# Two small joins of triangular inverses, moved from the attention's start to the stretch before it

## The chip, the cores and the metric

The program runs on one core of a Trainium2 chip, in one launch. Its engines are TensorE (PE, matmuls into PSUM; its weight loads are listed as PEld), VectorE (DVE), ScalarE (ACT), GpSimd (POOL) and SyncE (SP); 16 DMA engines move data, and transfers are issued here from SyncE's, ScalarE's and GpSimd's queues. A queue takes its instructions in order. The metric is the device time of one execution in microseconds (us); less is better.

## What is computed

One layer of a streaming encoder over 1024 tokens of width 1024: a half-step SwiGLU FFN, then two groups of heads side by side (latent attention of 4 heads, and an RWKV-7 recurrence of 8 heads of 64), then a second half-step FFN and a norm. Cut to what matters:

```python
kv = (rmsnorm(p_kv, kv_norm_g) @ w_ukv).reshape(B, S, MLA_HEADS, MLA_NOPE + MLA_V)
k_nope, v = kv[..., :MLA_NOPE], kv[..., MLA_NOPE:]
...
def step(state, inp):                      # RWKV-7, one token
    r_t, w_t, k_t, v_t, aa_t, bb_t = inp
    sa = jnp.einsum('bhvk,bhk->bhv', state, aa_t)
    state = (state * w_t[:, :, None, :] + sa[..., None] * bb_t[:, :, None, :]
             + v_t[..., None] * k_t[:, :, None, :])
    return state, jnp.einsum('bhvk,bhk->bhv', state, r_t)
```

## The kernel before

The recurrence is done in 16 chunks of 64 tokens, taken as 8 pairs of chunks. Within a chunk the recurrence needs the inverse of a 64x64 unit triangular matrix for each head. The kernel makes the two 32x32 diagonal blocks of every inverse on VectorE (`inverse32`, called once for each half of the heads), and stores them to DRAM: the first block in `tD` and, transposed, both in `fD`. The off-diagonal block of `fD` is made later, for one pair of chunks at a time, by `inverse(k, pool, p)`, called a join here. A join loads the off-diagonal block of the matrix (from `xD` into an `x21` tile) and both diagonal blocks (from `tD` into `T11`, from `fD` into `T22`), multiplies `x21` with `T11` (16 small matmuls), copies the product from PSUM into `w1`, multiplies with `T22` (16 more), copies again and stores the block into `fD`. All its transfers are issued from ScalarE's queue. The profile names tiles without their numbers, so `T11`, `T22` and the tile `T12` of the result all show as `T`, `x210` and `x211` as `x`, and `w1` as `w`; the PSUM tile is `ps_t`. Each product appears as 32 matmul instructions.

A pair's whole inverse is then loaded from `fD` into a `TF` tile by `Pair` (SyncE's queue, L1464), and `chain` uses it: a product `ps_z<-vu,m`, its copy `Z`, then the product `ps_z<-Z,TF`. The chain of a pair needs the state that the pair before leaves.

The work around the change stands in this order in the program: the latent projections (`mla_in`); `mla_up`, which makes queries, keys and, in its last two tasks, the values (`value`, PSUM tile `ps_v`, 8 blocks of tokens for each half of the value columns, copied out by ScalarE); the attention's first steps (`attend(0.4)`); the joins of pairs 0 and 1; `chain_tools` (memsets and copies on GpSimd for the chain's tiles `m`, `TF`, `wl`); and a loop over the 8 pairs, which mixes the chain of pair p, the join of pair p+2, the loads of pair p+1 and shares of the attention's steps. The attention's scores (`ps_s`) need the queries of a block as two tiles, `qh` (a ScalarE cast, L1224) and `ql` (a GpSimd subtraction, L1225).

The order of the program is a priority: a planner goes through the instructions at build time with its own cost model, and gives each engine the instruction that it takes for ready and that comes first. Pieces marked with a high priority (the chain, `inverse32`) go ahead. On the chip the order of each queue is then fixed. Tiles of one pool may lie where a pool that was closed before had its own; they wait for the last reader of what lay there.

Of the kernel before, what the change touches and what calls it, by code (L numbers as in the profile page):

```python
# [13 lines left out]
F32 = mybir.dt.float32  # L14
# [8 lines left out]
P = 128  # L23
# [47 lines left out]
def banks(k, **names):  # L71

    for n, b in names.items():
        turn = itertools.cycle(b)
        k.bank.update((x, turn) for x in n.split("_"))


def ps(k, name):
    b = next(k.bank[name])
    return k.psum.tile([P, HB], F32, name="ps_" + name, tag=f"bank{b}", bufs=1)  # L80
# [207 lines left out]
def empty():  # L288
    return [[None, None] for _ in range(ND)]
# [434 lines left out]
HL = L // 2  # L724
# [418 lines left out]
    return v(hi), v(lo)  # L1143


def mla_up(k, pool, wpool, att):

    nc = k.nc  # L1150
# [54 lines left out]
    for i, (f, h) in enumerate(tasks):  # L1205
        if i + 1 < len(tasks):
            ws.append(weights(*tasks[i + 1]))
        f(ws.pop(0), h)
    for a in range(2):
        split(k, k.krot[a], k.kr[0, a], k.kr[1, a])  # L1210
# [128 lines left out]

def inverse_tools(k, pool):  # L1340
    nc = k.nc
    k.T11, k.T22 = (pool.tile([P, 8, 2, HL], F32, name=n) for n in ("T11", "T22"))
    k.w1 = pool.tile([P, 8, HL], F32, name="w1")
    k.x21 = [pool.tile([P, 8, HL], F32, name=f"x21{i}") for i in range(2)]
    for t in [k.T11, k.T22, k.w1] + k.x21:
        nc.gpsimd.memset(t, 0.0)


# [28 lines left out]
def inverse(k, pool, p):  # L1377

    nc = k.nc
    x = k.x21[p % 2]  # L1380
    low = lambda e: slice(64 - 64 * e, 96 - 64 * e)
    high = lambda e: slice(96 - 64 * e, 128 - 64 * e)
    at = lambda e: slice(2 * p + e, 8 * NCH, NCH)
    for e in range(2):
        nc.scalar.dma_start(out=x[low(e)], in_=k.xD[at(e), :HL, HL:].rearrange("h s t -> s h t"))
        nc.scalar.dma_start(out=k.T11[low(e), :, e], in_=k.tD[at(e)].rearrange("h t c -> t h c"))
        nc.scalar.dma_start(out=k.T22[high(e), :, e], in_=k.fD[at(e), HL:, HL:].rearrange("h t c -> t h c"))

    def products(rows, lhs, rhs):
        t = ps(k, "t")[:, : 8 * HL].rearrange("p (h q) -> p h q", q=HL)  # L1390
        for h in range(8):
            for e in range(2):
                nc.tensor.matmul(t[rows(e), h], lhsT=lhs[:, h], rhs=rhs[:, h, e], start=True, stop=True)
        return t

    t = products(high, x, k.T11)
    for e in range(2):
        nc.scalar.copy(out=k.w1[high(e)], in_=t[high(e)])
    t = products(low, k.w1, k.T22)
    y = pool.tile([P, 8, HL], F32, name="T12", tag="T12", bufs=1)  # L1400
    for e in range(2):
        nc.scalar.copy(out=y[low(e)], in_=t[low(e)])
        nc.scalar.dma_start(out=k.fD[at(e), :HL, HL:].rearrange("h t c -> t h c"), in_=y[low(e)])
# [265 lines left out]
def tile_layer(ctx, tc, I, out):  # L1669
    k = Ctx()  # L1670
    setup(ctx, k, tc, I, out)
    nc = k.nc
    pool_ = lambda name, side="right": tc.tile_pool(name=name, bufs=1, side=side, reuse_waits="tile")
# [9 lines left out]
    with pool_("ffn1") as pool:  # L1683
# [5 lines left out]
        h = empty()  # L1689
# [61 lines left out]
        x = []  # L1751
# [65 lines left out]
    with pool_("winw", "left") as wpool:  # L1817
        with pool_("prep") as pool:
            win_rwkv(k, u2, pool, wpool, first)
        qkv = es_q.enter_context(pool_("qkv"))  # L1820
# [3 lines left out]

    es_a = ExitStack()
    att = es_a.enter_context(pool_("att", "left"))
    with pool_("upw") as pool:
        mla_up(k, qkv, pool, att)
    es_q.close()
    es_h.close()  # L1830
    ap = es_a.enter_context(pool_("attn", "left"))
# [6 lines left out]
    def attend(share):  # L1838
        nonlocal spent
        while steps and spent < share * total:  # L1840
            spent += cost.pop(0)
            steps.pop(0)()

    with pool_("inv", "left") as ip, pool_("chain") as pool:
        attend(0.4)
        inverse_tools(k, ip)
        inverse(k, ip, 0)
        inverse(k, ip, 1)
        chain_tools(k, pool)
        ops = [Pair(k, pool, 0)]  # L1850
        for hh in range(2):
            nc.gpsimd.memset(ops[0].sv(0, hh)[rows_of(0, hh)[1]], 0.0)
        late = None
        for p in range(NP2):
            o = ops.pop(0)
            even, odd, norm, gate = outputs(k, pool, o)
            with tc.high_priority(offset=1500):
                chain(k, pool, o, None, 0)
            if p + 2 < NP2:
                inverse(k, ip, p + 2)  # L1860
            if late:
                late()
            if p + 1 < NP2:
                ops.append(Pair(k, pool, p + 1))
            attend((p + 0.45) / 9.2)
            with tc.high_priority(offset=1500):
                chain(k, pool, o, ops[0] if ops else None, 1)
            with tc.high_priority(offset=0):
                even()
            attend((p + 1.21) / 9.2)  # L1870

            def late(odd=odd, norm=norm, gate=gate):
                with tc.high_priority(offset=0):
                    odd()
                    norm()
                    gate()

        late()
# [3 lines left out]
    h, y, u = empty(), empty(), {}  # L1882
# [3 lines left out]
    pool = Pools((own("h2b"), h0), (own("w2"), ("raw", "f8", "f9", "f10", "f11", "nwy", "nwt")))  # L1886
# [22 lines left out]
    x = []  # L1909
# [97 lines left out]
```

## Time and profile before

| | us |
|---|---|
| median of 3 runs | 2055.62 (2051.99 to 2059.74) |
| the profiled execution | 2057.89 |
| its span, first to last instruction | 2056.1 |
| TensorE busy | 1979.9 (96%) |
| VectorE busy | 1535.4 (75%) |
| ScalarE busy | 888.1 (43%) |
| GpSimd busy | 266.8 (13%) |

Times in the rows count from the start of the span. Busy time leaves out the issuing of transfers and the waiting in a queue. The granted clock (PEclk) is TensorE's as a share of 2.4 GHz: 1.00, or 0.50 for the lower level, 1.2 GHz, or a mean over a stretch.

### The profile page before, as it was taken

How to read it: one execution, taken by the hardware profiler on the slowest of the kernel's cores; microseconds unless marked ns; L12 is line 12 of the kernel's file. 1: busy time of each engine (PE TensorE's matmuls, PEld its weight loads, DVE VectorE, ACT ScalarE, POOL GpSimd, SP SyncE). 2: the span in 40 equal slices, each digit the busy share in tenths (PEclk: the TensorE clock that was granted, in tenths of full speed). 3: DMA queues.
4: the chain of work that ended last, by engine and by line, in shares of the span. 5: the costliest groups of instructions: out<-in, count | busy, mean ns of one | idle time of the engine just before them, and what ended most of it. 6: DMA issues, size and time to landing. Idle time of an engine off the chain costs nothing.

```text
span 2056.1 us, 29503 instructions
## 1 busy us (share of the span) xinstructions
PE 1979.9 (96%) x10648; PEld 1594.1 (78%) x10648; DVE 1535.4 (75%) x2939; ACT 888.1 (43%) x1678; POOL 266.8 (13%) x319
## 2 busy tenths in 40 slices
PE   6999999999999999999978899999999999999997
PEld 4788888887888777767867787787888888888887
DVE  6999997659996577896665766568566665699975
ACT  5633334335443464543344444455333333354433
POOL 1100000001000244532132323211000000000001
PEclk8999999999999999999998999999999999999999
DMA  8277753347452124656338874741223223375412
GB/s 340 78 250 236 266 177 115 111 156 248 166 175 88 67 57 122 164 136 163 88 88 175 186 184 130 266 159 42 84 85 108 103 97 106 118 269 189 144 62 83
DMA packets 222611, 302.13 MB, mean 147 GB/s; under 512 B 104704, under 2 KB 138880, under 8 KB 222464
## 3 DMA queue, kind: packets, MB, share of 16 engines
q1 hardware_dynamic: 195280, 280.16, 43.6%
q0 software_dynamic: 5120, 15.73, 2.4%
q10 hardware_dynamic: 22064, 4.35, 1.2%
q8 instruction: 84, 1.38, 0.3%
q14 instruction: 63, 0.52, 0.1%
HBM read 216.81 MB, written 80.74 MB: 145 GB/s over the span
## 4 chain that ended last, share of the span: by engine, by line
PE 71%; DVE 13%; DMA 7%; issue 4%; ACT 2%; POOL 1%; SPq 0%; DVEq 0%; ACTq 0%; POOLq 0%
PE ps_w L68 35%; PE ps_dn L68 20%; PE ps_in L68 4%; PE ps_wo L68 4%; DVE pair L62 2%; DVE wmod L140 1%; PE ps_s L68 1%; DVE T L1369 1%; PE ps_ov L1274 1%; DVE Tpr L1365 1%; DMA wmod<-w_mod 1%; PE ps_y L1519 1%; PE ps_z L1485 1%; DMA hraw<-hidD 1%; PE ps_pt L1266 1%
## 5 line engine op out<-in xcount | busy, mean ns | idle before, releaser
L68 PE MATMUL ps_w<-pair 128*128 128x512 f32 x3744 | 873.8, 394 | 13.8 <-ACT pair L61 10.2
L68 PEld LDWEIGHTS ps_w<-pair 128*128 128x128 f32 x3744 | 704.3, 188 | 180.4 <-ACT pair L61 11.5
L68 PE MATMUL ps_dn<-pair 128*128 128x512 f32 x1512 | 351.1, 393 | 1.4 <-ACT pair L61 0.6
L68 PEld LDWEIGHTS ps_dn<-pair 128*128 128x128 f32 x1512 | 283.3, 188 | 68.2 <-ACT pair L61 1.4
L68 PE MATMUL ps_in<-pair,win 128*128 128x512 f32 x960 | 239.4, 402 | 2.9 <-ACT pair L282 2.2
L61 ACT CAST pair<-raw 128x512 fp32r<-128x512 f32 x256 | 153.8, 621 | 179.6 <-PE ps_w L68 102.3
L68 PEld LDWEIGHTS ps_in<-pair,win 128*128 128x128 f32 x960 | 179.6, 190 | 50.8 <-issue 9.3
L62 DVE TENSOR_TENSOR pair<-raw,pair 128x512 fp32r<-128x512 f32 x256 | 175.5, 698 | 40.3 <-ACT pair L61 40.2
L570 DVE SCALAR_TENSOR_TENSOR h<-ps_dn,mod,h 128x512 f32<-128x512 f32 (+1 forms) x208 | 148.4, 726 | 47.4 <-PE ps_dn L68 47.4
L400 ACT COPY part<-ps_w 128x512 f32<-128x512 f32 x120 | 70.4, 586 | 210.3 <-PE ps_w L68 193.9
L61 ACT CAST pair<-draw 128x256 fp32r<-128x256 f32 x216 | 77.6, 403 | 103.3 <-DMA draw<-ffn_w_down 55.4
L61 ACT CAST pair<-hraw 128x512 fp32r<-128x512 f32 x142 | 85.6, 619 | 80.2 <-PE ps_dn L68 31.8
L62 DVE TENSOR_TENSOR pair<-hraw,pair 128x512 fp32r<-128x512 f32 x142 | 95.3, 685 | 15.5 <-ACT pair L61 15.3
L502 DVE TENSOR_TENSOR t<-ps_w,part 128x512 f32<-128x512 f32 x80 | 53.9, 686 | 55.7 <-ACT part L400 45.6
L62 DVE TENSOR_TENSOR pair<-draw,pair 128x256 fp32r<-128x256 f32 x216 | 83.6, 418 | 4.3 <-ACT pair L61 4.2
L140 DVE SCALAR_TENSOR_TENSOR wmod<-wmod,cact 128x1024 f32<-128x1024 f32 x68 | 82.8, 1220 | 4.1 <-DMA wmod<-w_mod 3.9
L68 PE MATMUL ps_dn<-pair,dh 128*128 128x512 f32 (+1 forms) x320 | 83.7, 350 | 0.0
L497 DVE TENSOR_TENSOR c<-ps_w,part 128x512 f32<-128x512 f32 x80 | 53.5, 686 | 39.3 <-ACT part L400 31.9
L68 PE MATMUL ps_wo<-pair,woh 128*128 128x512 f32 x256 | 79.3, 391 | 0.2 <-ACT woh L61 0.2
L498 ACT ACTIVATE c<-c 128x512 f32<-128x512 f32 x80 | 49.2, 630 | 40.2 <-DVE c L497 39.3
L319 POOL DMA_DIRECT2D h<-x x16 | 8.7, 549 | 436.9 <-ACT part L400 385.0
L319 POOL DMA_DIRECT2D h<-hD x16 | 8.6, 541 | 436.6 <-ACT part L400 364.6
(352 smaller groups left out, 2820.4 us busy)
## 6 DMA issues: line engine op xcount, KB each, us to landing
wmod<-w_mod SPq DMA_DIRECT2D x68, 512.0 KB, 4.4
raw<-ffn_w_gate SPq DMA_DIRECT2D x44, 512.0 KB, 4.3
raw<-ffn_w_up SPq DMA_DIRECT2D x44, 512.0 KB, 4.3
hidD<-c SPq DMA_DIRECT2D x44, 512.0 KB, 3.3
draw<-ffn_w_down SPq DMA_DIRECT2D x44, 512.0 KB, 5.0
hraw<-hidD SPq DMA_DIRECT2D x72, 256.0 KB, 3.1
hD<-h SPq DMA_DIRECT2D x32, 256.0 KB, 2.0
m3D<-m SPq DMA_DIRECT2D x32, 256.0 KB, 4.6
```

What stands on the lines that cost most here:

```text
L61: k.nc.scalar.copy(out=hi, in_=src)
L62: k.nc.vector.tensor_tensor(out=lo, in0=src, in1=hi.bitcast(F32), op=ALU.subtract)
L68: k.nc.tensor.matmul(out, lhsT=x, rhs=y, start=start, stop=stop, skip_group_check=onto)
L140: k.nc.vector.scalar_tensor_tensor(out=w, in0=w, scalar=1.0, in1=k.cact, op0=ALU.mult, op1=ALU.mult, accum_out=m)
L400: nc.scalar.copy(out=t, in_=x)
L497: nc.vector.tensor_tensor(out=c[i][:, j], in0=x, in1=y, op=ALU.add)
L498: nc.scalar.activation(out=c[i][:, j], in_=c[i][:, j], func=AF.Silu)
L502: nc.vector.tensor_tensor(out=t, in0=x, in1=y, op=ALU.add)
L570: nc.vector.scalar_tensor_tensor(out=y, in0=x, scalar=gt[:, d : d + 1], in1=y, op0=ALU.mult, op1=ALU.add)
L1266: nc.tensor.transpose(tp[:, q : q + P], pr[:, s0 + q : s0 + q + P], k.ident)
L1274: nc.tensor.matmul(x.po[:, cols], lhsT=pt[:, b * P : (b + 1) * P], rhs=k.v[b][:, cols], start=b == 0, stop=b == x.i)
L1365: nc.vector.tensor_tensor(out=v, in0=T[:, t, 0:m][:, None, :].broadcast_to([P, n, m]), in1=xp[:, t, m:][:, :, None].broadcast_to([P, n, m] ...
```

## The change

The joins of pairs 0 and 1 are called from `mla_up`, ahead of its first task for the values. The pool of their tiles is opened before `mla_up` and stays open until the attention's tiles are closed. `T11` and `T22` become one tile, `TT`: the first block is loaded into its rows `low(e)`, the second into its rows `high(e)`; in the first product the rows of `x21` that meet the second block are zero, in the second those of `w1` that meet the first. One `x21` tile serves all pairs instead of two in turn. The PSUM bank for `ps_t` is the same, 4.

```diff
-def mla_up(k, pool, wpool, att):
+def mla_up(k, pool, wpool, att, joins):
...
+        if (f, h) == (value, 0):
+            joins()
         f(ws.pop(0), h)
...
 def inverse_tools(k, pool):
     nc = k.nc
-    k.T11, k.T22 = (pool.tile([P, 8, 2, HL], F32, name=n) for n in ("T11", "T22"))
-    k.w1 = pool.tile([P, 8, HL], F32, name="w1")
-    k.x21 = [pool.tile([P, 8, HL], F32, name=f"x21{i}") for i in range(2)]
-    for t in [k.T11, k.T22, k.w1] + k.x21:
+    k.TT = pool.tile([P, 8, 2, HL], F32, name="TT")
+    k.w1, k.x21 = (pool.tile([P, 8, HL], F32, name=n) for n in ("w1", "x21"))
+    for t in [k.TT, k.w1, k.x21]:
         nc.gpsimd.memset(t, 0.0)
...
-    x = k.x21[p % 2]
+    x = k.x21
...
-        nc.scalar.dma_start(out=k.T11[low(e), :, e], in_=k.tD[at(e)].rearrange("h t c -> t h c"))
-        nc.scalar.dma_start(out=k.T22[high(e), :, e], in_=k.fD[at(e), HL:, HL:].rearrange("h t c -> t h c"))
+        nc.scalar.dma_start(out=k.TT[low(e), :, e], in_=k.tD[at(e)].rearrange("h t c -> t h c"))
+        nc.scalar.dma_start(out=k.TT[high(e), :, e], in_=k.fD[at(e), HL:, HL:].rearrange("h t c -> t h c"))
...
-    t = products(high, x, k.T11)
+    t = products(high, x, k.TT)
...
-    t = products(low, k.w1, k.T22)
+    t = products(low, k.w1, k.TT)
...
     att = es_a.enter_context(pool_("att", "left"))
+    ip = es_a.enter_context(pool_("inv", "left"))
+    inverse_tools(k, ip)
+    banks(k, t="4")
+
+    def joins():
+        for p in range(2):
+            inverse(k, ip, p)
+
     with pool_("upw") as pool:
-        mla_up(k, qkv, pool, att)
+        mla_up(k, qkv, pool, att, joins)
...
-    with pool_("inv", "left") as ip, pool_("chain") as pool:
+    with pool_("chain") as pool:
         attend(0.4)
-        inverse_tools(k, ip)
-        inverse(k, ip, 0)
-        inverse(k, ip, 1)
         chain_tools(k, pool)
```

## Rows read from the trace of the kernel before

**Rows 1.** The page, its first part: busy time, share of the span, instructions.

```profile
PE 1979.9 (96%) x10648; PEld 1594.1 (78%) x10648; DVE 1535.4 (75%) x2939; ACT 888.1 (43%) x1678; POOL 266.8 (13%) x319
```

**Rows 2.** Stretches: length, busy time of each engine (instructions), PEclk, DMA share, GB/s.

```profile
1061.00:1075.00 14.00, 12.73 (x98) 11.74 (x96) 4.39 (x7) 10.37 (x22) 0.51 (x2) 1.00 0.02 5
1075.00:1081.00 6.00, 0.74 (x4) 0.53 (x4) 0.00 (x0) 0.96 (x2) 5.53 (x18) 0.93 0.79 168
1081.00:1090.00 9.00, 7.38 (x74) 6.51 (x76) 3.49 (x16) 4.22 (x11) 6.02 (x11) 0.50 1.00 191
...
1104.10:1107.40 3.30, 3.30 (x46) 2.79 (x48) 0.65 (x3) 1.57 (x5) 0.00 (x0) 0.50 0.93 230
...
1162.10:1260.00 97.90, 97.22 (x1372) 80.06 (x1370) 68.07 (x253) 43.57 (x110) 25.57 (x31) 1.00 0.68 161
```

**Rows 3.** Timeline of TensorE: start, length, instruction, [idle before it <- what ended that].

```profile
1081.50 0.29 PE L1393 MATMUL ps_t<-T,x 128*32 128x32 f32 x2 [5.27 <-DMA x<-xD]
...
1098.00 0.70 PE L1393 MATMUL ps_t<-T,w 128*32 128x32 f32 x32 [0.98 <-ACT w L1398]
...
1101.87 0.33 PE L1485 MATMUL ps_z<-Z,TF 128*64 128x64 f32 x2 [2.03 <-DMA TF<-fD]
...
1104.01 1.10 PE L1485 MATMUL ps_z<-Z,TF 128*64 128x64 f32 x14 [0.59 <-DMA TF<-fD]
...
1110.61 0.25 PE L1393 MATMUL ps_t<-T,w 128*32 128x32 f32 x2 [0.89 <-DMA T<-fD]
```

**Rows 4.** SyncE's queue in the timeline, and the view of line L1374.

```profile
1051.44 3.08 SPq L1374 DMA_DIRECT2D fD<-Tpr  x2
...
1099.23 2.72 SPq L1464 DMA_DIRECT2D TF<-fD  x4
...
L1374 SPq DMA_DIRECT2D fD<-Tpr x4: 599/1217/2397, 947.5 to 1052.1; - x4
...
DMA to landing us min/median/max: 4.1/4.7/6.7
```

**Rows 5.** Timeline of GpSimd, 1074 to 1085 us.

```profile
1074.49 0.99 POOL L1346 MEMSET T<- 128x512 f32 x2 [17.02 <-PE ps_v L68]
1075.41 0.31 POOL L1346 MEMSET w<- 128x256 f32 x1
1075.67 0.57 POOL L1346 MEMSET x<- 128x256 f32 x2
1076.18 0.21 POOL L1414 COPY wl<-WL 64x32 f32<-64x32 f32 x1
...
1078.72 0.21 POOL L1414 COPY wl<-WL 64x32 f32<-64x32 f32 x1
1079.01 1.26 POOL L1225 TENSOR_TENSOR ql<-q,qh 128x512 fp32r<-128x512 f32 x1
...
1082.40 1.85 POOL L1418 MEMSET TF<- 128x1024 f32 x2
```

**Rows 6.** Instructions on ps_t alone, one stretch: length, busy PE, PEld, ACT, PEclk.

```profile
1075.00:1100.00 25.00, 4.05 (x128) 3.21 (x128) 2.18 (x6) 0.80 0.84 171
```

**Rows 7.** The views of ps_t (first row) and of line L1387: ns min/median/max.

```profile
L1398 ACT COPY w<-ps_t x16: 363/365/367, 1085.9 to 1207.5; 32x256 f32<-32x256 f32 x16
...
L1387 ACTq DMA_DIRECT2D T<-fD x16: 309/312/517, 1075.5 to 1190.9; - x16
...
DMA to landing us min/median/max: 1.9/3.4/9.2
```

**Rows 8.** ScalarE and its queue in the timeline, and one wait of TensorE.

```profile
1145.46 0.34 ACTq L1386 DMA_DIRECT2D T<-tD  x1
...
1151.82 3.19 ACTq L1387 DMA_DIRECT2D T<-fD  x2
...
1157.42 0.78 ACT L1253 ACTIVATE pr<-ps_s,st,qs 128x512 f32<-128x512 f32 x1 [6.91 <-DMA T<-fD]
...
1158.34 0.96 PE L68 MATMUL ps_s<-kn,qh 128*128 128x512 f32 x2 [2.63 <-ACT pr L1253]
```

## The prediction

> **What bounds the kernel now.** The page comes first: TensorE is busy 96% of the span [rows 1], so a change that lets some step be ready earlier is worth only the TensorE idle time, and the slowly clocked time, that this step causes now. Then the view by stretches shows where that time is [rows 2]. The values' projection (1061 to 1075 us) is nearly dense on TensorE at full clock, with the DMA engines at a share of 0.02. Right behind it, 1075 to 1081 us, TensorE works 0.74 of 6 us, and the next 9 us are granted half the clock (0.50, the 1.2 GHz level) with the DMA engines full. A second half-clock piece lies at 1104.1 to 1107.4 us. From 1162 to 1260 us TensorE is busy 97.22 of 97.90 us: whatever is saved before moves the end by as much, because nothing is idle there to absorb it. The timeline of TensorE then tells who ended its waits between 1074 and 1112 us [rows 3]: a join's x21 load 5.27, a join's ScalarE copy 0.98, the load of the finished inverse (TF) 2.03 and 0.59, a join's second diagonal block 0.89. All of them are put down to the first joins, or to what reads them.
>
> **What the change moves.** Two calls of inverse() go from behind the first attention steps to ahead of the first half of the values' projection. Each brings 6 ScalarE-issued loads, two products of 16 small matmuls (32 instructions each in the trace), 4 ScalarE copies and 2 ScalarE-issued stores; the memsets of their tiles move along on GpSimd.
>
> *Waits that go.* With the joins stored before the attention starts, the copy wait (0.98), the two TF waits (2.03 and 0.59) and the block load wait (0.89) lose their cause: 4.49 us [rows 3]. The TF load of pair 0 is issued now at 1099.23 us, when the join's store has landed [rows 4]; then it is the TF memset, at 1082.40 with 1.85 us [rows 5], that it waits for, so it is out some 15 us earlier. If the inverse is not what is late, the operands' loads are next; TensorE has attention steps to run meanwhile, and I count nothing for them.
>
> *Clock.* The half-clock piece at 1104.1 us comes right after the 2.03 and 0.59 us waits; TensorE works all its 3.30 us [rows 2, 3]. Without the waits I take it at full clock, half the time: 1.65 us.
>
> *TensorE's own work.* The joins of pairs 0 and 1 take 4.05 us of TensorE now, part of it at half clock [rows 6]. At full clock 32 of these matmuls take 0.70 us [rows 3], the row at 1098.00, so four sets in the values' stretch take 2.80: a gain of 1.25 us.
>
> *The first wait.* The 5.27 us before 1081.50 are booked to the x21 load. The scores' next matmul needs ql, which GpSimd begins at 1079.01 and ends at 1080.27, because from 1074.49 on it does the joins' memsets (0.99, 0.31, 0.57) and then the chain's [rows 5]. So the join is not alone late here; ql is 1.2 us behind it. If GpSimd keeps its order, taking out 1.87 us of memsets brings ql forward by that, and TensorE resumes 3.1 us earlier (1.2 and 1.87). If the order is made again, the chain's other memsets (1.85 for TF alone) can slip in ahead of ql and it comes up to 1.2 us later than the present resumption. I take 0, between the ends: GpSimd goes from the joins' memsets to the chain's without a gap, from 1076.18 to 1078.93 [rows 5], so the room that is freed can be filled by the next ones in the same way.
>
> *What it costs in the values' stretch.* Nothing of before shows a join there, so bounds. From below, 0: the stretch has 12.73 us of matmuls that need no join [rows 2], and if the queue has them between the joins' steps, everything is covered. From above: the second diagonal blocks come from a store issued at 1052.1 us (the second of two, which begin at 1051.44) that lands 6.7 us later at most, at 1058.8 [rows 4]; the loads take 3.4 us to land at the median [rows 7], thus 1062.2, against a stretch that begins at 1061.0: the first product is 1.2 us late. Pair 1 now shares x21 and TT with pair 0, and its loads can't start before pair 0's second product: 3.4 us more, and four copy waits of 0.98, in all 8.5 us if nothing lies between. ScalarE's ledger: it is busy 10.37 of 14 us here [rows 2], 3.6 spare; eight copies of 0.365 are 2.9 us, and ten issues (pair 1's loads, all four stores) of 0.31 are 3.1 [rows 7]. That is 2.4 over, against 2.8 of added matmul time: just covered, if the order is good. I take 3.0 us, nearer to the lower bound, because the same kind of waits cost 0.98 and 0.89 each among the attention steps, where other work lay between.
>
> *One tile for two blocks.* In later pairs the T11 loads, issued now right after the first product of the pair before, wait for its second. Behind them on ScalarE's queue stand the attention's exponentials and the chain's copies; TensorE waits for those. Now there is one such block: two loads, held up from 1151.82 on, keep an exponential waiting 6.91 us and TensorE 2.63 us [rows 8]. But the first product in before has its tile of the second block loaded last as well in these pairs (from 1151.82 on, against 1145.46 for T11), and the join can't finish without it. So I take 0; its cover is the attention work that keeps TensorE busy from 1162 us on [rows 2], and without that cover it would cost a TF wait, 2.03 us, for each of six pairs.
>
> The Trainium skill (Perfetto Trace Analysis, "DMA Instruction — HWDGE") says that on this chip the issuing sequencer itself waits for the semaphores before a DMA starts, which speaks against more dependent loads on ScalarE's queue; the 6.91 us of [rows 8] agree.
>
> **The sum.** 2056.1 − 4.49 − 1.65 − 1.25 + 0 + 3.0 = 2051.7 us of span, 4.4 less. The profiled execution took 2057.89 us, 1.8 around its span, and would take 2053.5; the median of the runs is 2055.62 and becomes 2051.2, in round figures 2051.
>
> The best sum has no stall and the 3.1 us at the first wait, and the 9 us at half clock partly back: of the 7.38 us busy there the joins had at most their 4.05, the rest, 3.3 at least, would take half, 1.7 less. 2055.62 − 7.4 − 3.1 − 1.7 is 2043.4. The worst of the forecast's own case is −7.4 + 8.5 + 1.2, and one half-clock piece of 3.3 us at half worth, 1.65: 2059.6.
>
> **Rivals.** *ScalarE's queue is held (slower).* A load of the second block stands in ScalarE's queue ahead of the casts for the last keys, and waits for the landing at 1058.8 from 1054.5 on, when SyncE has issued the store (1051.44 and 3.08) [rows 4]. For: loads did hold that queue [rows 8]. Against: up to 1061 us ScalarE has room, and keys' casts could stand ahead. Price 4.3 us before the values and 8.5 in them: 12.8 − 7.4 = 5.4 slower, 2061. It decides from a total stall of 7.4 us on. Chance 0.15. What the Trainium skill says of the sequencer's wait, named above, is the rule behind this case; by it the time would be those 2061.
>
> *The joins stay behind the values.* The instructions are ordered at build by a planner with its own times; if it takes T for late, the two joins land at the end of the values' stretch and run there. For: T's second store does land at 1058.8, and the values' stretch begins 2.2 us later. Against: loads only need an idle queue. Only the memsets are gained: 1.87 at most, less some stall: 2055. Chance 0.15.
>
> *The first wait goes too (faster).* ql leaves GpSimd early and TensorE comes back before the clock is lowered: 2043, the best sum above. For: the joins' memsets are first in that queue [rows 5]. Against: the chain's own operations still stand there, 2.75 us of them ahead of ql already. Chance 0.15.
>
> **Chances and range.** The forecast keeps 0.55. Half a per cent, about what a measurement of this kernel tells from no change, is 10.3 us: under 2045.3 or over 2065.9. Faster by that is most of the last rival, 0.11, and a tail of the forecast, 0.04: 0.15. Slower by that needs the first rival with half as much again, or a reordering further on that no row shows: 0.07. Within: 0.78. The range 2042 to 2062 runs from the last rival's time to the first rival's, with a microsecond more at either end.
>
> **What would show it.** Right: the joins' first matmuls between 1058 and 1066 us, the pair-0 store landed before the values end, the TF load of pair 0 issued within some 12 us of their end, no TensorE wait on TF before 1110 us, no half clock at 1104 us, the values' stretch 3 to 6 us longer. The first wait is still there, now released by ql. Wrong: TensorE waits of more than 7 us between 1050 and 1080 us; a new half-clock piece there; joins after the last value matmul; or an idle TensorE between 1162 and 1260 us, which would mean that the later joins have become late.

## The result, and the profile after

The changed kernel takes 2070.39 us (median of 6 runs, 2066.88 to 2073.02); the kernel before, run beside it, 2056.82 (6 runs, 2051.99 to 2062.15). The ratio is 1.0058, 95% interval 1.0043 to 1.0073: slower by 13.6 us, and outside the forecast's range. The profiled execution took 2073.02 us with a span of 2071.2. The page's first part, as in [rows 1], tells next to nothing: TensorE's share is the same, 2.2 us more are busy in a span that is 15.1 us longer.

```profile
PE 1982.1 (96%) x10648; PEld 1597.5 (77%) x10648; DVE 1534.4 (74%) x2939; ACT 886.7 (43%) x1678; POOL 264.3 (13%) x317
```

To find the place, three stretches counted from the last matmul of the queries and keys (`ps_uq`), which ends at 1061.38 us before and at 1062.46 after: the first 200 us (joins, chain, attention), the next 40 (the end of attention), the next 70 (the out projection). The view by stretches, columns as in [rows 2]; first the kernel before:

```profile
1061.38:1261.38 200.00, 181.73 (x2535) 152.81 (x2536) 121.89 (x442) 91.49 (x229) 56.03 (x81) 0.96 0.70 157
1261.38:1301.38 40.00, 33.88 (x215) 27.55 (x215) 26.82 (x87) 19.81 (x37) 13.09 (x21) 1.00 0.72 255
1301.38:1371.38 70.00, 69.82 (x315) 57.35 (x314) 45.37 (x55) 38.11 (x56) 15.76 (x10) 1.00 0.55 177
```

The changed kernel:

```profile
1062.46:1262.46 200.00, 181.53 (x2536) 153.96 (x2536) 123.18 (x454) 88.50 (x223) 56.59 (x78) 0.94 0.71 165
1262.46:1302.46 40.00, 37.62 (x216) 31.21 (x215) 24.75 (x61) 19.93 (x37) 7.67 (x13) 1.00 0.61 204
1302.46:1372.46 70.00, 55.73 (x260) 45.43 (x259) 31.98 (x50) 29.11 (x44) 17.41 (x16) 0.88 0.45 147
```

In the first 200 us, where the whole change lies, TensorE is as busy as before (181.53 against 181.73) and gets through as many matmuls (2536 against 2535): nothing was gained there. In the next 40 it is busy 3.74 us more, in the last 70 it is busy 14.09 us less, and at a lower clock (0.88). The loss is made in the third stretch, 240 us behind the joins. (The rows are of one profiled execution of each kernel. The runs of the kernel before lie up to 10 us apart, so a microsecond or two between two executions says little.)

What happens there needs a word on the code. The out projection has two halves of 512 tokens, each of 8 tiles with 24 matmuls into `ps_wo`. The second half reads attention's output, which each block of 128 queries sends through DRAM: four transpositions (`ps_ot`), a ScalarE copy (`ot`), a store into `oD`, then loads (`yraw`), casts (`pair`), and the first weight's cast (`woh`). The program mixes the last five attention steps with the first tiles of the first half. The timeline of the changed kernel, all engines (SPq and ACTq are the DMA queues), where the last block is sent:

```profile
1325.10 0.72 ACT L1290 ACTIVATE o<-o,oss 128x512 f32<-128x512 f32 x1 [2.92 <-DVE oss L249]
...
1330.76 0.60 PE L1296 MATMUL ps_ot<-ident,o 128*128 128x128 f32 x4
1331.12 0.70 PE L68 MATMUL ps_wo<-pair,woh 128*128 128x512 f32 x2
1331.40 0.59 ACT L1298 COPY ot<-ps_ot 128x512 f32<-128x512 f32 x1 [5.57 <-PE ps_ot L1296]
1331.66 0.40 PE L68 MATMUL ps_wo<-pair,wol 128*128 128x512 f32 x1
1332.01 0.52 ACTq L1300 DMA_DIRECT2D oD<-ot  x1
...
1334.82 0.80 SPq L1577 DMA_DIRECT2D yraw<-oD  x2
...
1341.88 2.37 ACT L61 CAST pair<-yraw 128x512 fp32r<-128x512 f32 x4 [0.17 <-DMA yraw<-ybD]
...
1345.21 1.03 ACT L61 CAST woh<-wo 128x1024 fp32r<-128x1024 f32 x1
...
1346.29 1.22 PE L68 MATMUL ps_wo<-pair,woh 128*128 128x512 f32 x2 [14.23 <-ACT woh L61]
```

The block's output is ready at 1325.82 (1325.10 and 0.72), but TensorE does its transpositions only at 1330.76, behind matmuls of the out projection that stand ahead of them in its queue. Then the way through DRAM starts, and TensorE has 3 matmuls left. It waits 14.23 us, and then works its first microseconds at half clock. Counted from the end of `ps_uq`, the second half starts 10.4 us later than before. The Trainium skill (PSUM — Partial Sum Buffer, "Engine vs sequencer instructions") says that matmuls start and complete in program order; the trace agrees, 4.94 us for operands that were ready.

In the kernel before the same transpositions, copy and store come 36 us earlier, and the loads are issued while the first half runs until 1334.8; TensorE stays busy across the border (timeline, then the stretch):

```profile
1294.88 0.60 PE L1294 MATMUL ps_ot<-ident,o 128*128 128x128 f32 x4
...
1296.16 0.52 ACTq L1298 DMA_DIRECT2D oD<-ot  x1
...
1310.23 0.33 SPq L1575 DMA_DIRECT2D yraw<-oD  x1
```

```profile
1329.30:1352.00 22.70, 22.70 (x107) 18.69 (x107) 11.09 (x13) 9.46 (x12) 5.26 (x4) 1.00 0.52 175
```

In TensorE's order the last transpositions stand behind 24 of the first half's 192 matmuls before, and behind 189 after. What stands ahead of them has changed too. The chain's last instructions on TensorE (`ps_yt`, transpositions of its output) stand 20 instructions behind attention's last score before, and 71 ahead of it after. The views of both tiles, first before, then after (ns min/median/max, then first and last start):

```profile
L1553 PE MATMUL ps_yt<-ident,yc x64: 272/273/323, 1140.2 to 1274.7; 128*64 128x128 f32 x64
L1242 PE MATMUL ps_s<-kr,qr x48: 278/389/628, 1082.3 to 1273.1; 128*128 128x512 f32 x24, 128*128 128x256 f32 x16, 128*128 128x384 f32 x8
...
L1555 PE MATMUL ps_yt<-ident,yc x64: 272/273/323, 1127.2 to 1263.6; 128*64 128x128 f32 x64
L1244 PE MATMUL ps_s<-kr,qr x48: 278/389/416, 1089.5 to 1277.4; 128*128 128x512 f32 x24, 128*128 128x256 f32 x16, 128*128 128x384 f32 x8
```

The joins themselves moved as forecast. The timeline of the changed kernel from their first product to the first load of TF, all engines; its waits answer to [rows 3], its GpSimd lines to [rows 5]:

```profile
1062.57 0.85 PE L1395 MATMUL ps_t<-TT,x 128*32 128x32 f32 x32
...
1066.59 0.91 ACTq L1405 DMA_DIRECT2D fD<-T  x2
...
1069.08 0.39 PE L68 MATMUL ps_v<-uh,kvh 128*128 128x256 f32 x1 [0.66 <-ACT v L1198]
...
1071.44 0.66 PE L1395 MATMUL ps_t<-TT,x 128*32 128x32 f32 x30 [0.67 <-DMA TT<-fD]
...
1081.22 0.66 PE L1395 MATMUL ps_t<-TT,x 128*32 128x32 f32 x30 [0.86 <-DMA TT<-fD]
...
1086.09 1.25 POOL L1227 TENSOR_TENSOR ql<-q,qh 128x512 fp32r<-128x512 f32 x1
...
1087.49 0.29 PEld L1521 LDWEIGHTS ps_y<-vu,m 128*64 128x64 f32 x2 [4.19 <-POOL ql L1227]
1087.53 0.45 PE L1521 MATMUL ps_y<-vu,m 128*64 128x64 f32 x2 [4.11 <-DMA TT<-fD]
...
1089.13 2.90 SPq L1466 DMA_DIRECT2D TF<-fD  x4
```

The waits of [rows 3] on TF are gone, TF is loaded ten microseconds earlier, and the store of the pair-0 block is issued inside the values' stretch (`ps_v` from 1063.35 to 1080.36). But other waits stand there, of 0.66, 0.67 and 0.86 us, and 4.11 us ahead of 1087.53. The last is put down to a load that had let a join go on 6 us before, so another thing came last: the weight load of the same matmul is put down to GpSimd's `ql`, which ends at 1087.34, and in e2, below, the same wait to GpSimd's clear of `vu`. The stretches, to be read beside [rows 2]:

```profile
1063.30:1080.30 17.00, 15.10 (x201) 13.85 (x195) 2.29 (x4) 10.30 (x25) 0.21 (x1) 1.00 0.21 33
...
1084.85:1101.92 17.07, 13.10 (x111) 11.23 (x113) 5.40 (x25) 5.96 (x17) 6.51 (x10) 0.50 0.96 203
...
1104.00:1107.40 3.40, 3.40 (x56) 2.90 (x55) 3.22 (x13) 2.02 (x7) 0.62 (x1) 1.00 1.05 219
...
1112.16:1115.57 3.41, 3.41 (x42) 2.96 (x44) 0.84 (x2) 0.25 (x2) 1.23 (x2) 0.50 0.40 108
1136.05:1139.46 3.41, 3.41 (x55) 2.58 (x53) 1.02 (x2) 2.10 (x5) 0.58 (x1) 0.50 1.11 234
1162.10:1260.00 97.90, 94.79 (x1306) 80.38 (x1306) 71.16 (x266) 43.85 (x111) 27.68 (x33) 1.00 0.69 171
```

No half clock lies at 1104 now, but there are pieces of the same length at 1112.16 and 1136.05, and the one behind the values is 17.07 us long. The stretch from 1162.10 to 1260 us, where TensorE was idle 0.68 us before [rows 2], has 3.11 us idle.

### The profile page after: what moved, and what is told of

It reads as the page before. It is cut to its first block, busy times and chain, and to the rows that moved or that the text cites. A ratio compares the mean times of both kernels' runs of the same rounds, so it can differ in the third digit from the quotient of the medians.

```text
span 2071.2 us, 29509 instructions
## 1 busy us (share of the span) xinstructions
PE 1982.1 (96%) x10648; PEld 1597.5 (77%) x10648; DVE 1534.4 (74%) x2939; ACT 886.7 (43%) x1678; POOL 264.3 (13%) x317
## 4 chain that ended last, share of the span: by engine, by line
PE 73%; DVE 11%; DMA 7%; ACT 3%; issue 3%; SPq 1%; POOL 1%; ACTq 0%; DVEq 0%; POOLq 0%
PE ps_w L68 39%; PE ps_dn L68 20%; PE ps_in L68 4%; PE ps_wo L68 4%; DVE pair L62 1%; DVE T L1371 1%; DVE Tpr L1367 1%; PE ps_ov L1276 1%; PE ps_s L68 1%; DMA m3D<-m 1%; DVE wmod L140 1%; DMA hraw<-hidD 1%; DMA oD<-ot 1%; PE ps_pt L1268 1%; DMA TF<-fD 1%
## 5 line engine op out<-in xcount | busy, mean ns | idle before, releaser
L68 PEld LDWEIGHTS ps_dn<-pair 128*128 128x128 f32 x1512 | 283.1, 188 | 69.9 <-DVE h L570 1.9
L68 PEld LDWEIGHTS ps_wo<-pair,woh 128*128 128x128 f32 x256 | 48.5, 192 | 25.1 <-ACT woh L61 15.2
```

Of the source, the lines that this page charges most:

```text
L68: k.nc.tensor.matmul(out, lhsT=x, rhs=y, start=start, stop=stop, skip_group_check=onto)
```

## The experiments

The theory to test: the planner, given a chain that it expects earlier, mixes attention's tail with the out projection; the way through DRAM is then uncovered, and that is the loss, while the early joins are worth little. The rivals: the single tiles hold up ScalarE's queue; the pool's place; the joins' place itself. Times were taken in five rounds beside the kernel before, whose medians were 2057.2 to 2059.3. "Behind" is the number of matmuls of the out projection's first half (of 192) ahead of attention's last transpositions; "wait" is TensorE's wait ahead of the second half; "second half" is its start, counted from the end of `ps_uq`, in the profiled execution. e13 to e15 leave work out.

| run | median us | ratio [95%] | behind | wait | second half |
|---|---|---|---|---|---|
| kernel before | 2057 to 2059 | 1 | 24 | 0 | 273.4 |
| changed kernel | 2070.39 | 1.0058 [1.0043, 1.0073] | 189 | 14.23 | 283.8 |
| e1_tail_first | 2065.09 | 1.0033 [1.0019, 1.0047] | 153 | 8.14 | 275.4 |
| e2_tail_bank | 2057.13 | 0.9999 [0.9988, 1.001] | 93 | 0 | 272.1 |
| e3_tail_before_all | 2058.56 | 1.0009 [0.9998, 1.002] | 24 | 0 | 272.0 |
| e4_joins_late_pool_early | 2094.16 | 1.0182 [1.0165, 1.0198] | 192 | 14.76 | 306.3 |
| e5_clear_on_vector | 2058.19 | 1.0 [0.999, 1.001] | 24 | 0 | 277.1 |
| e6_before_clear_on_vector | 2060.83 | 1.0024 [1.0012, 1.0037] | 24 | 0 | 280.8 |
| e7_one_tile_alone | 2066.24 | 1.0044 [1.0029, 1.0058] | 22 | 0 | 288.0 |
| e8_one_join_early | 2065.41 | 1.0044 [1.0028, 1.0059] | 93 | 0 | 280.5 |
| e9_early_separate_tiles | 2055.83 | 0.9993 [0.998, 1.0005] | 24 | 0 | 269.2 |
| e10_one_diagonal_tile | 2065.09 | 1.0038 [1.0023, 1.0053] | 22 | 0 | 280.7 |
| e11_one_offdiagonal_tile | 2066.42 | 1.0047 [1.0029, 1.0066] | 22 | 0 | 283.1 |
| e12_third_join_after_chain | 2069.19 | 1.0043 [1.0031, 1.0055] | 90 | 0 | 277.1 |
| e13_two_joins_left_out | 2060.35 | 1.0009 [0.9996, 1.0021] | 146 | 7.11 | 272.8 |
| e14_left_out_banks_5_3 | 2060.40 | 1.0005 [0.9994, 1.0016] | 69 | 0 | 267.3 |
| e15_left_out_banks_3_2 | 2053.15 | 0.9967 [0.9956, 0.9979] | 24 | 0 | 268.9 |

**The tail.** The changed kernel with one edit, then a second one that makes the out projection's tiles wait for a PSUM bank of attention:

```diff
     for d in range(early):
-        while len(steps) > early - d:
+        while steps:
             steps.pop(0)()
...
-    banks(k, wo="56")
+    banks(k, wo="53")
```

e1 has the first edit alone, e2 both, e3 both with "32" for "53".

> The changed kernel, with all five remaining attention steps emitted ahead of the first tile of the out projection instead of one ahead of each of the first five tiles. In the planned order of TensorE the last transposition of attention's output then stands behind 153 of the first half's 192 matmuls, instead of 189. Main theory (the loss is made where attention's tail meets the out projection: the second half's operands pass through DRAM, which took 14.9 us from the last transposition at 1331.36 to the first matmul at 1346.29, with only 3 matmuls left to cover it): 36 more matmuls of about 0.27 us cover some 10 us of it, so TensorE's wait ahead of the second half shrinks from 14.2 to 4 to 6 us, and the time is 2056 to 2062. Rival (the joins' place, the single buffers or the pool's place cost the time somewhere else): the wait is a symptom, and the time stays within 3 us of 2070.

> As the run before it, and the out projection's second PSUM tile shares the bank of attention's output tile (banks 5 and 3 in turn instead of 5 and 6), so that from the second tile on it has to wait until attention's output is read out. The last transposition then stands behind 93 of the 192 matmuls, and 99 matmuls of about 0.27 us (27 us) lie behind it. Main theory: the 14.9 us through DRAM are covered whole, no wait over 2 us and no half clock ahead of the second half; the kernel keeps the 3 to 4.5 us by which the changed kernel was ahead when the first half ran out: 2050 to 2055. Rival (the loss lies elsewhere): 2067 to 2073.

> As the two runs before it, but the out projection's tiles use banks 3 and 2, those of attention's output and of its transposition, so that no matmul of the out projection runs before attention's values are done; the last transposition stands behind 24 matmuls, as in the kernel before. Main theory: no wait ahead of the second half, but the gaps of attention's last steps are no longer filled (the scores end at 1277.8, and the steps behind them took 13.4 us in the kernel before), so the first tile starts near 1289 to 1291, some 10 us later than in the changed kernel and 2 to 4 us later than in the kernel before: 2057 to 2063, slower than the run with banks 5 and 3. Rival (the loss lies elsewhere): at or above 2070.

The four orders of the same work go as the main theory says: 189, 153, 93 and 24 matmuls ahead of the transpositions, waits of 14.23, 8.14, 0 and 0. With the tail in order the 13 us are gone. Timelines of TensorE, first e1, then e2, which has no wait over 1 us from there to the second half:

```profile
1318.98 0.60 PE L1296 MATMUL ps_ot<-ident,o 128*128 128x128 f32 x4
...
1336.61 0.79 PE L68 MATMUL ps_wo<-pair,woh 128*128 128x512 f32 x1 [8.14 <-ACT woh L61]
```

```profile
1304.42 0.60 PE L1296 MATMUL ps_ot<-ident,o 128*128 128x128 f32 x4
```

In e1 the way from the end of the transpositions (1319.58) to the second half took 17.0 us, 2.1 more than in the changed kernel, and the 39 matmuls that cover it took 0.23 us each, not 0.27. So it missed its expectation (a wait of 4 to 6 us, 2056 to 2062). e2 missed its expectation: it is at the kernel before's time, not 3 to 4.5 us under it. The lead that I counted on did not come from the joins: it is the 3.74 us of busy time in the second stretch, where matmuls of the out projection fill the gaps of attention's last steps. e3, which forbids that, has 33.91 us there again, as the kernel before, and is at its time all the same, as I had expected:

```profile
1059.76:1259.76 200.00, 181.42 (x2556) 154.25 (x2557) 123.70 (x455) 90.22 (x228) 56.80 (x78) 0.95 0.71 165
1259.76:1299.76 40.00, 33.91 (x201) 28.19 (x200) 24.09 (x74) 19.51 (x38) 10.55 (x18) 1.00 0.68 224
```

**Joins called late, pool early.**

```diff
-        if (f, h) == (value, 0):
-            joins()
...
         attend(0.4)
+        joins()
```

> The changed kernel with the two joins' calls put back behind attention's first share, where they stood; the pool of the joins' tiles still opens early, its memsets are still early and it still lives until attention is done. In the planned order the last transposition stands behind all 192 matmuls of the first half. Main theory (the order at the tail decides, wherever the joins are): the wait ahead of the second half is 14 to 16 us, and the time is 2070 to 2076, with no early joins at all. Rival 1 (the joins' place ahead of the values costs the time, by the 5.9 us later end of the values or by queues on ScalarE): near 2057. Rival 2 (the pool's place alone changes nothing): near 2057 too, with the tail ahead of the out projection.

It doesn't tell rival 1 apart, since the joins didn't move: their first product starts at 1064.77, ahead of the first matmul for the values (1065.38). Their pool is open and their tiles are cleared, and it seems that the planner then takes them as soon as their loads allow; e8's second join, called late as well, also runs inside the values' stretch. The loss is larger than I expected, and only in part of the same kind: the scores too stand between the out projection's tiles and end at 1317.61 instead of 1277.79, and the first 200 us alone have 26.47 us of TensorE's idle time, 18.27 in the kernel before.

```profile
1355.64 0.66 PE L1294 MATMUL ps_ot<-ident,o 128*128 128x128 f32 x4 [3.65 <-ACT o L1288]
...
1371.06 0.79 PE L68 MATMUL ps_wo<-pair,woh 128*128 128x512 f32 x1 [14.76 <-ACT woh L61]
```

**The first wait.** The clears of the chain's tiles go from GpSimd to VectorE, in the changed kernel (e5) and in the kernel before (e6).

```diff
-                k.nc.gpsimd.memset(m[u, 2 * hh + e, 0], 0.0)
+                k.nc.vector.memset(m[u, 2 * hh + e, 0], 0.0)
     for t in k.TF:
-        k.nc.gpsimd.memset(t, 0.0)
+        k.nc.vector.memset(t, 0.0)
```

> The changed kernel, with the clears of the chain's tiles (eight of 64x256 and two of 128x1024, some 6 us together on GpSimd between the values' end and the first ql) put on VectorE, which does nothing for some 20 us there. The planned order of TensorE then has attention's last transposition behind 24 matmuls of the out projection again, though the joins are as early as in the changed kernel and the tail is not touched. Main theory (the planned order at the tail made the loss, and the early joins themselves are worth little): no wait ahead of the second half, the 4.1 us wait behind the values shrinks to under 2.5 us, and the time is 2049 to 2056. Rival (early joins or the single tile cost the time, by queues on ScalarE): 2065 or more.

> The kernel before with the same clears on VectorE: the joins stay behind the values. It tells what of the run before it comes from the clears. Main theory: the 5.27 us wait behind the values becomes 2 to 4 us (the joins' own loads and clears still stand there), the tail is in order as before: 2053 to 2058, and the changed kernel with the same clears is 1 to 5 us below it, which would be what the early joins are worth once the tail is in order. Rival (early joins are worth nothing): both within 1 us of each other.

In e5 the tail comes out in order though nothing of it was edited, and the loss is gone with it. The wait behind the values is not: it was 4.11 us and is 4.00, now for a load of the chain's own tiles.

```profile
1088.12 0.45 PE L1521 MATMUL ps_y<-vu,m 128*64 128x64 f32 x2 [4.00 <-DMA m<-arD]
```

Both are above what I had expected. e5 lies 2.6 us under e6, inside the 1 to 5 us that early joins should then be worth; but the planner made another order for each, so that the difference is not the joins' alone. e5 also shows that early joins, one tile and an early pool together don't force the tail into disorder: in its order the chain's last `ps_yt` stand 20 instructions behind the last score again, as in the kernel before.

**One tile.** The kernel before, the joins where they stood: one diagonal tile (e10, the first diff), one off-diagonal tile (e11, the second), both as in the change (e7).

```diff
-    k.T11, k.T22 = (pool.tile([P, 8, 2, HL], F32, name=n) for n in ("T11", "T22"))
+    k.T11 = k.T22 = pool.tile([P, 8, 2, HL], F32, name="TT")
```

```diff
-    k.x21 = [pool.tile([P, 8, HL], F32, name=f"x21{i}") for i in range(2)]
+    k.x21 = [pool.tile([P, 8, HL], F32, name="x21")] * 2
```

> The kernel before with the one tile for both diagonal blocks and the one tile for the off-diagonal block, and the joins and their pool where they stood. Main theory: a load has to wait for the join before it, which the traces show covered (stores land well ahead); 2056 to 2060, no change to 3 us. Rival (the single buffers hold up ScalarE's queue, 6 joins times some 2 us): 2065 to 2070.

> The kernel before with one tile for both diagonal blocks and still two tiles in turn for the off-diagonal block. If the second product's block held up the next join's loads (in the run with both single tiles the second join's block loads were issued at 1091.5 to 1093.6, behind the first join's copies, and landed at 1099.5; in the kernel before from 1084.9 on), most of the 8.8 us is here: 2062 to 2067. If it is the off-diagonal tile: 2056 to 2059.

> The kernel before with one tile for the off-diagonal block instead of two in turn, and separate tiles for the diagonal blocks. Counterpart of the run before it: 2056 to 2059 if the diagonal tile carries the cost, 2062 to 2067 if this one does; if both are at 2058 to 2062, each carries part.

Each costs 8 to 10 us and both together no more. e7 came out in its rival's range, not in the main theory's; e10 and e11 each in the range for "this tile carries the cost", which can't hold for both if costs add. In e7 the second join's block is loaded behind the first join's stores, and TensorE stands ahead of its product (ScalarE's queue, then TensorE; the row books the wait to "issue", so that it ends with the landing is not shown):

```profile
1090.56 0.84 ACTq L1402 DMA_DIRECT2D fD<-T  x1
1091.50 0.66 ACTq L1386 DMA_DIRECT2D TT<-fD  x1
...
1099.34 0.28 PE L1392 MATMUL ps_t<-TT,x 128*32 128x32 f32 x2 [3.33 <-issue]
```

The first 200 us of e7 and of e10:

```profile
1057.27:1257.27 200.00, 177.17 (x2384) 148.20 (x2382) 114.49 (x420) 88.22 (x220) 53.55 (x77) 0.92 0.70 153
```

```profile
1059.53:1259.53 200.00, 181.67 (x2447) 152.87 (x2448) 121.01 (x430) 90.31 (x227) 53.83 (x78) 0.92 0.71 157
```

e7 is 151 matmuls behind the kernel before, e10 88, with the busy time of before: there it is the clock (0.92 against 0.96). The three share a later chain in TensorE's order: its last product (`ps_z`) stands 2500 to 2513 instructions behind `ps_uq`, 2452 in the kernel before. But each has waits of its own as well: 2.25 and 2.46 us for loads into `TT` in e7, 2.92 and 1.56 in e10, 4.57 for `TF` in e11. Which of the two makes the cost was not tested further.

**What early joins are worth.** e8 is e2 with the first join alone ahead of the values:

```diff
-        for p in range(2):
-            inverse(k, ip, p)
+        inverse(k, ip, 0)
...
         attend(0.4)
+        inverse(k, ip, 1)
```

e9 is the changed kernel with `inverse_tools` and `inverse` of the kernel before (`T11`, `T22`, two `x21`), called with the values' pool for the first two joins and with the old pool for the rest:

```diff
-            inverse(k, ip, p)
+            inverse(k, pool, p)
...
     with pool_("upw") as pool:
+        inverse_tools(k, pool)
...
-    with pool_("chain") as pool:
+    with pool_("inv", "left") as ip, pool_("chain") as pool:
         attend(0.4)
+        inverse_tools(k, ip)
```

e12 is e9 with both edits of e2 and a lower priority for the later joins:

```diff
-                inverse(k, ip, p + 2)
+                with tc.high_priority(offset=-300):
+                    inverse(k, ip, p + 2)
```

> As the run with banks 5 and 3 for the out projection, but only the first join is called ahead of the values; the second is called where it stood. The tail is in order (93 matmuls). If it is the joins' work inside the values' stretch that gives the gain back (values' end 5 to 6 us later for a chain that starts no earlier), the time is 2 to 3 us below that run: 2053 to 2056. If the planner moves the second join up anyway, because its tiles are there, nothing changes: 2056 to 2058.

> The first two joins ahead of the values' projection as in the changed kernel, but with separate tiles: two for the diagonal blocks and two in turn for the off-diagonal block, for the first two joins in the pool of the values' projection, and for the other six in the pool that they had in the kernel before (so its clears are made twice, and that pool closes with the chain again). In the planned order the last transposition stands behind 24 matmuls. The run with one tile alone cost 8.8 us, those with early joins, one tile and an ordered tail cost nothing. Theory A (the costs add: one tile +9, early joins -9, disordered tail +13): 2046 to 2051. Theory B (a single tile costs nothing once the first two joins are early, and early joins gain nothing): 2055 to 2059. Theory C (early joins lose by the values' stretch and the second set of clears): 2060 or more.

> Early joins with separate tiles as in the run before these, with the later joins at a lower priority, so that the third join's second product stands behind the chain's first ones, and the out projection's tiles on banks 5 and 3 (the last transposition behind 90 matmuls). An attempt at a version that beats both. If the wait for the third join's block (5.34 us ahead of its first product) is what holds up the chain's start and with it the rest, the wait shrinks and the time is 2050 to 2054; if TensorE merely waits at the next place, because the chain's own loads land no earlier (the chain's first product stood 30.2 us behind the queries' last matmul there, 27.5 us in the kernel before), 2055 to 2059.

e9 is the early joins without the two things that cost: 1.4 us faster at the middle, between 4.1 faster and 1.0 slower, which can't be told from no change. That is theory B; the costs of the parts don't add. Its tail is in order, and the chain's last `ps_yt` stand 20 instructions behind the last score, as in e5. Its first stretch has 1.7 us less idle time than that of the kernel before, and one wait has taken the place of the first one of [rows 3], 5.34 us for the third join's block (stretch, then timeline):

```profile
1061.91:1261.91 200.00, 183.46 (x2547) 154.38 (x2547) 125.55 (x453) 91.58 (x231) 57.43 (x82) 0.96 0.72 159
```

```profile
1084.42 0.28 PE L1396 MATMUL ps_t<-T,x 128*32 128x32 f32 x2 [5.34 <-DMA T<-tD]
```

e8 and e12 missed both of their expectations, 8 to 10 us slower with the tail covered. e8's first 200 us have 22.81 us of idle time (18.51 in e2), 4.89 of it in one wait ahead of a product of the chain, booked to "issue"; its cause stays open. e12's second half starts 3.7 us later than in the kernel before, and it waits once more where the feed-forward part begins, in an order that differs there too (5.86 us, then half clock):

```profile
1414.75 2.07 PE L68 MATMUL ps_w<-pair 128*128 128x512 f32 x4 [4.04 <-ACT pair L61]
1418.64 1.65 PE L68 MATMUL ps_w<-pair 128*128 128x512 f32 x3 [1.82 <-DVE pair L62]
```

**Two joins left out.** The kernel before without the first two joins (zeros are stored early in place of their blocks), in three orders.

```diff
+    zero = att.tile([P, 8, HL], F32, name="zero")
+    nc.gpsimd.memset(zero, 0.0)
+    for j in range(4):
+        nc.scalar.dma_start(out=k.fD[slice(j, 8 * NCH, NCH), :HL, HL:].rearrange("h t c -> t h c"), in_=zero[:HL])
...
-        inverse(k, ip, 0)
-        inverse(k, ip, 1)
```

> The kernel before with the joins of pairs 0 and 1 left out altogether (their blocks of the inverse are stored as zeros, from a cleared tile, ahead of the values), so that the chain never waits for them and TensorE has 4 us of work less: the bound of what any earlier place of these two joins can give. The order is left to the planner, which puts the last transposition behind 146 of the first half's 192 matmuls. Main theory (an earlier chain makes the planner spread attention's tail over the out projection, and that costs more than the joins can give): 2058 to 2065, slower than the kernel before with work left out, with a wait of 5 to 9 us ahead of the second half. Rival (the disorder comes from the one tile or the pool, not from the earlier chain): no wait there and 2048 to 2053.

> The same with the out projection's tiles on banks 5 and 3 and the remaining attention steps emitted first (last transposition behind 69 matmuls). Without the tail's wait this is what the two joins cost where they stood. If the forecast's 4.4 us and the 2.8 us of matmuls that it left in are all to be had: 2049 to 2052. If other waits take the place of the joins' (as idle time of TensorE in the runs with early joins suggests, 1 to 1.7 us less instead of 4.49): 2053 to 2056.

> The same with banks 3 and 2 (last transposition behind 24 matmuls, as in the kernel before), a second order of the same work, to see how far the order alone moves the time: within 2 us of the run with banks 5 and 3 by both theories.

e13 has neither the one tile nor the early pool, only a chain that is not held up, and its tail is in disorder: work is taken out, and the kernel isn't faster. e15 has the same work with the tail in front and is 7.2 us below it. So neither the one tile nor the early pool is needed for the disorder. Early joins don't suffice for it either (e5, e9). What goes with it in every order here is where the planner puts the chain's end. In the kernel before, e5 to e7 and e9 to e11 the last `ps_yt` stand 20 instructions behind the last score, and only 22 or 24 matmuls of the out projection come before the last transpositions. In the other ten they stand 50 to 210 ahead of it, and 69 matmuls or more come before, unless the out projection's tiles are on banks 3 and 2 (e3, e15: 24). That is a pattern of 17 orders; why the planner puts the chain's end where it does was not looked into. e14, which should have been as good as e15, waits where the feed-forward part begins, like e12 (4.04 and 1.81 us, then half clock), and gives back what it had won; its second half starts 6.1 us earlier than in the kernel before. The wait of e13 in the timeline of TensorE:

```profile
1336.64 0.80 PE L68 MATMUL ps_wo<-pair,woh 128*128 128x512 f32 x1 [7.11 <-ACT woh L61]
```

e15, which by its expectation should have been within 2 us of e14, is the best of the three: 6.8 us (4.3 to 9.1) below the kernel before, 2.8 of it matmuls that any place must pay (four sets of 0.70, [rows 3]). So in this order an earlier place could give some 4 us, not the 7.4 that the forecast set against 3.0 of cost. It is no strict bound: another order might give more, and the edits at the tail (steps first, banks 3 and 2) were not run on the kernel before with its joins, so that their own share in the 6.8 us is not known. No version with the whole work beats the kernel before by more than its interval; e9 comes nearest.

## Why the prediction was wrong

**The step that failed** is the sentence that whatever is saved before moves the end by as much, because from 1162 to 1260 us nothing is idle [rows 2]; the sum rests on it, and has no term for what lies behind 1260 us. That holds for a fixed order. Here the order was made again from the planner's estimates, for everything behind the joins. In its place the runs showed three things: on balance nothing was saved in the first 200 us (next paragraph), the stretch itself has 3.11 us idle instead of 0.68, and a new wait of 14.23 us stands at 1332, with half-clock work behind it. Ordering the tail alone takes the 13 us away (e2, e3). The text names "a reordering further on that no row shows" among the slow cases, with a chance of 0.07 that no row supports. A row of the kernel before at that border would have shown a way through DRAM and its cover (the last `ot` store 39 us ahead of the second half); it needs 15 to 18 us (14.9 in the changed kernel, 17.0 in e1, 17.6 in e13).

**Waits that go, 4.49 us.** They went, but TensorE's idle time in the first 200 us did not: 18.27 us before (200.00 less 181.73), 18.47 after. The in-order queues waited for the next thing that was late: the third join's loads, ScalarE's copies in the values' stretch, the chain's own loads, clears and steps. The step priced waits by their rows as if each were removed with its cause. This is the second step that failed: with the tail in order (e2, e3) the time is that of the kernel before, not the 4.4 us less of the forecast. Even with two joins left out altogether the idle time of those 200 us is not less (19.03, 19.73 and 21.57 us in e13 to e15). TF was loaded ten microseconds earlier, not 15: not its clear, which was done at 1085.4, but loads of `m` stood ahead of it in SyncE's queue until 1089.0.

**Clock, 1.65.** The piece at 1104 us went, as said (granted clock 1.00 at 1104.0 to 1107.4), but nothing came of it: half-clock pieces of 3.41 us lie at 1112.16 and 1136.05 (in the kernel before at 1104.06 and 1158.67). The piece behind the values grew from 10.24 to 17.07 us in the profiled execution, and the first 200 us have a mean of 0.94 instead of 0.96.

**The joins' own work, 1.25.** In order of size right: all matmuls of the joins between 1062.5 and 1088.2 took 4.81 us for 194, thus 3.17 for the 128 of two joins, against 4.05 before [rows 6] and 2.80 forecast.

**The first wait, 0.** Near: 5.27 before, 4.11 after, a gain of 1.2 us. That GpSimd's queue would fill the freed room was right too: `ql` starts at 1086.09, 5.7 us behind the values' end at 1080.36; in e5, with the clears off GpSimd, the wait stays at 4.00 us for a load.

**The values' stretch, 3.0.** It is 4.3 us longer (17.01 against 12.75, first to last `ps_v`). But 2.57 us of that are the joins' matmuls, which the sum counts in the term before; TensorE is idle 1.90 us in it, 0.40 before. So the stall came out at 1.5 to 1.7 us, inside the bounds and under the 3.0; a part of a third join lies in it, which I had not put there.

**One tile, 0.** Not shown wrong for the changed kernel as a whole: e2 has it, e9 has not, and their intervals overlap. But a later join's load into `TT` keeps TensorE waiting 1.59 us at 1195.39, in the stretch that was to cover it. At the joins' old place it costs 8 to 10 us (e7, e10, e11), so the cover that I named, attention's work from 1162 us on, doesn't hold there. The uncovered price in the text, 2.03 for each of six pairs, is 12.2, of the same order; the waits of these runs are not those six, so that is luck.

**The rivals.** None came true. ScalarE's queue was not held ahead of the values: no wait of TensorE over 1.4 us from 1050 to 1080. The joins did not stay behind, and the first wait did not go. The signs listed as right nearly all came, which is the lesson: they were all signs of the mechanism near the edit, and none looked at the next border. Of the signs of being wrong one came in part, the idle time between 1162 and 1260 us.

What stays open: how the planner's order depends on each edit (e5 puts the tail in order by moving clears), what the tail's edits would do to the kernel before, what in e7, e10 and e11 lowers the clock and the pace together, and what costs e8 and e12 their 8 to 10 us.

## What to carry to other kernels

Where the order of the queues is made at build time from estimates, an edit that makes one stage ready earlier can change the order at the next borders too: look there for transfers through DRAM, count how much of TensorE's work stands behind the last producer, and compare it with the time of the way (15 us here, 189 of 192 matmuls gone). Bind such an order with a dependency, as the shared PSUM bank did in e2 and e3, before an edit is judged by its time. And bound a gain by leaving the work out: with two joins gone, three orders gave 2053 to 2060 us, a spread larger than the gain that was sought.

## What the runs showed of the hardware

The granted clock stayed at 0.50 for 17.07 us from 1084.85 on, though TensorE worked 13.10 of them; after the 14.23 us wait it was again 0.50 for 17.07 us, with TensorE idle for the first 12 and only 4.76 us of work in it:

```profile
1334.02:1351.09 17.07, 4.76 (x10) 3.31 (x11) 7.28 (x10) 10.11 (x16) 8.46 (x6) 0.50 0.87 292
```

So the length of such a piece is no measure of what it costs: the second one cost some 2.4 us of work at half speed, and the idle time 14.2.
